# Another ring of score buffers, another order of batch 0, and another ending in a gather and scatter kernel

## The chip, the cores and the metric

The kernel runs on one core of one Trainium2 chip. The metric is device microseconds of one execution. The kernel before takes 828.68 us as the median of 3 runs (828.26 to 828.69). Times inside the execution are counted from the start of the profiled span. VectorE (DVE), ScalarE (ACT), GpSimd (POOL), TensorE (PE) and SyncE (SP) have instruction queues of their own; transfers between memory and the core's buffers are moved by 16 DMA engines, which serve SP's queue and GpSimd's queue.

## The reference

There are B = 8 batches. `scores` has 8 x 2048 x 2048 float32 numbers (134 MB), `values` and the output have 8 x 2048 rows of 2560 float32 numbers (10,240 bytes a row).

```python
best_j = np.argmax(scores, axis=2)
gathered = values[b_idx, best_j, :].copy()
out = np.zeros_like(values)
np.add.at(out, (b_idx, best_j, slice(None)), gathered)
```

So output row j of batch b is `values[b, j]` times the number of score rows of that batch whose maximum stands in column j. A row that is chosen once is a plain copy of its values row, one that is never chosen is zeros, and one that is chosen twice or more is the values row times its count. With the inputs of this case, batch 0 has 748 rows of the first kind, 761 of the second and 539 of the third, and the other batches differ from these by a few per cent.

## The kernel before

**Scores to counts** (`count_steps`, L166). A row tile is 128 score rows, one per partition, so a batch has NT = 16 row tiles and the kernel 128 of them; in this text they are numbered 0 to 127. SP loads two row tiles at a time (R = 2, 2 MB, 16,384 bytes per partition; L181), the very first load alone in two halves. VectorE finds the maximum of each row (L188) and its column (L189). After every four row tiles it makes one-hot matrices of the columns (L194 to L202), and TensorE adds them up into the batch's counts (L207).

**Where the scores lie.** NB = 7 buffers of two row tiles each are a rotating pool (`spool`). At the start three more stand in `vbig`, the area of six rows per partition that later stages gathered rows. For the first 20 loads (row tiles 0 to 39) buffers are taken in turn from all ten, so 20 row tiles can be there at once; afterwards 14 can. A load waits until VectorE has finished the tiles that its buffer held.

**Counts to output rows** (`value_steps`, L272). After a batch's counts are there, VectorE makes three kinds of index list, and GpSimd issues indirect transfers with them, 128 list entries a piece; an entry out of bounds moves no row.

- Single rows: 16 copies from DRAM to DRAM (`copy_once`, L285, issued at L33), one for each 128 rows, with an index out of bounds where the row isn't a single one. They need only the counts (L275 to L282).
- Zero rows: `zeros` (L369) writes a row of zeros to up to 7 x 128 listed rows (12 lists in the last batch). The lists come from a ranking (L294 to L355) in which TensorE has two short parts.
- Rows chosen more than once: `gathers` (L359) fetches up to 5 x 128 values rows into slots of `vbig` (L150), ScalarE multiplies each by its count (L363), and a scatter writes them (L155). There are six slots, so a gather waits for the scatter that used its slot.

VectorE, TensorE, ScalarE and SP run in the order in which the program is written (`manual_schedule`, L395). `count_steps` and `value_steps` are generators: at each `yield` of the first, after one row tile, the main loop (L397 to L406) lets the second, of the batch before, go on to its own next `yield`. For batches 0 and 1 the main loop takes four steps of `value_steps` at once (L404), so that all lists are made before the next batch's first row tile. For batch 0 GpSimd's order is 6 copies, then 7 zero lists with 7 copies between them, then 5 gathers with the last 3 copies between them, then 5 scatters; the gathers need the three `vbig` buffers back from the score tiles, and ten `yield`s (L380) put them behind row tiles in program order. For later batches 6 (batch 1) or 4 copies go first.

**The end.** Copies, zero lists and the last six scatters are marked `free_running` (L141): the framework doesn't follow them, and each adds 16 to a semaphore `landed`. At the end GpSimd waits until all have landed and resets its DMA state (L454 to L456). A branch before it (L421) handles inputs whose lists overflow and isn't taken here.

Of the kernel before, what the change touches and what calls it, by code (L numbers as in the profile page):

```python
# [8 lines left out]
FP32 = mybir.dt.float32  # L9
# [5 lines left out]
P = 128  # L15
# [21 lines left out]
def kernel(  # L37
# [6 lines left out]
    nc = tc.nc  # L44
    B, S, S2 = scores.shape
    _, _, H = values.shape
    assert S == S2
    NT = S // P
    BIG = float(1 << 24)
    R = 2  # L50
    G = 4
    NV = 6
    NX = NV * H // (R * S)
    NB = 7
    NM = NT // 2
    NE = 16
    LE = P // NE
    ZCAP, MCAP = 7, 5
# [6 lines left out]
    last_row = nc.gpsimd.to_reg(B * S - 1)  # L65

    consts = ctx.enter_context(tc.tile_pool(name="consts", bufs=1))
    spool = ctx.enter_context(tc.tile_pool(name="spool", bufs=NB))
    small = ctx.enter_context(tc.tile_pool(name="small", bufs=3))
    fin = ctx.enter_context(tc.tile_pool(name="fin", bufs=2))  # L70
    ohp = ctx.enter_context(tc.tile_pool(name="ohp", bufs=1))
# [44 lines left out]
    zero1 = consts.tile([P, 1], FP32)  # L116
# [2 lines left out]
    zrow = ctx.enter_context(nc.sbuf_tensor([P, H], FP32))  # L119
    nc.scalar.copy(zrow[:], zero1[:].to_broadcast([P, H]))  # L120

    vbig = ctx.enter_context(nc.sbuf_tensor([P, NV * H], FP32))
    nc.scalar.copy(vbig[:, NX * R * S:NV * H], zero1[:].to_broadcast([P, NV * H - NX * R * S]))

    ones_i = ctx.enter_context(nc.sbuf_tensor([P, B * NT], INT32))
    zero_i = ctx.enter_context(nc.sbuf_tensor([P, B * NT], INT32))
# [11 lines left out]
    landed = tc.alloc_semaphore("landed")  # L138
    n_free = [0]
# [14 lines left out]
    def scatter(v, idx, note=writes_out):  # L154
        note(nc.gpsimd.indirect_dma_start(  # L155
            out=out_flat[:, :], out_offset=bass.IndirectOffsetOnAxis(ap=idx, axis=0),
            in_=v, in_offset=None, bounds_check=B * S - 1, oob_is_err=False))

    vslot = [0]

    def stage():
        v = vbig[:, vslot[0] * H:(vslot[0] + 1) * H]
        vslot[0] = (vslot[0] + 1) % NV
        return v

    def count_steps(b, cnt_ps):  # L166

        am = None
        for u in range(NT // R):
            x = b * NT // R + u  # L170
            if x < 2 * (NX + NB) and x % (NX + NB) < NX:
                x %= NX + NB
                s_tile = vbig[:, x * R * S:(x + 1) * R * S]
            else:
                s_tile = spool.tile([P, R * S], FP32, name="s_tile")[:]
            rows_in = scores[b, u * R * P:(u + 1) * R * P, :].rearrange("(p r) s -> p (r s)", r=R)

            parts = R if b == u == 0 else 1
            for r in range(parts):
                part = slice(r * R * S // parts, (r + 1) * R * S // parts)  # L180
                nc.sync.dma_start(out=s_tile[:, part], in_=rows_in[:, part])  # L181
            if u * R % G == 0:
                am = small.tile([P, G, 8], U32, name="am")
            for r in range(R):
                g = (u * R + r) % G
                rows = s_tile[:, r * S:(r + 1) * S]
                mx = small.tile([P, 8], FP32)
                nc.vector.max(out=mx[:], in_=rows)  # L188
                nc.vector.max_index(out=am[:, g, :], in_max=mx[:], in_values=rows)  # L189
                if g < G - 1:  # L190
                    yield
            if (u + 1) * R % G == 0:
                lo = small.tile([P, G], U32)
                nc.vector.tensor_single_scalar(out=lo[:], in_=am[:, :, 0], scalar=P - 1, op=ALU.bitwise_and)  # L194
                hi = small.tile([P, G], U32)
                nc.vector.tensor_single_scalar(out=hi[:], in_=am[:, :, 0], scalar=7, op=ALU.logical_shift_right)  # L196
                oh_lo = small.tile([P, G, P], BF16)
                nc.vector.tensor_tensor(  # L198
                    out=oh_lo[:], in0=lo[:].unsqueeze(2).to_broadcast([P, G, P]),
                    in1=lane_f[:].unsqueeze(1).to_broadcast([P, G, P]), op=ALU.is_equal)  # L200
                oh_hi = small.tile([P, G, NT], BF16)
                nc.vector.tensor_tensor(  # L202
                    out=oh_hi[:], in0=hi[:].unsqueeze(2).to_broadcast([P, G, NT]),
                    in1=lane_f[:, 0:NT].unsqueeze(1).to_broadcast([P, G, NT]), op=ALU.is_equal)
                for g in range(G):
                    t = (u + 1) * R - G + g
                    nc.tensor.matmul(out=cnt_ps[:], lhsT=oh_lo[:, g, :], rhs=oh_hi[:, g, :],  # L207
                                     start=(t == 0), stop=(t == NT - 1))
                yield

    def level_engines(rank):

# [59 lines left out]
    def value_steps(b, cnt_ps):  # L272
# [14 lines left out]
                nc, out_flat[:, :], values[b, t * P:(t + 1) * P, :], one_i[:, t:t + 1], last_row))  # L287


        first = 6 if b < 2 else 4  # L290
        for t in range(first):
            copy_once(t)

# [22 lines left out]
        if b == B - 1:  # L316
# [9 lines left out]
            out=oh[:], in0=lo[:].unsqueeze(2).to_broadcast([P, NT, P]),  # L326
# [4 lines left out]
            out=ez[:], in0=hi[:, 0, :].unsqueeze(2).to_broadcast([P, NT, NT]),  # L331
# [3 lines left out]
            out=em[:], in0=hi[:, 1, :].unsqueeze(2).to_broadcast([P, NT, NM]),  # L335
# [6 lines left out]
        for t in range(NT):  # L342
            nc.tensor.matmul(out=l_ps[:], lhsT=oh[:, t, :], rhs=put[:, t, :], start=(t == 0), stop=(t == NT - 1))  # L343
        yield
        yield

        mi = many_i[:, b * NM:(b + 1) * NM]
        mc = many_c[:, b * NM:(b + 1) * NM]
# [8 lines left out]
        staged = []  # L357

        def gathers():  # L359
            for k in range(MCAP):  # L360
                v = stage()
                gather(v, mi[:, k:k + 1])
                nc.scalar.activation(out=v, in_=v, func=mybir.ActivationFunctionType.Copy, bias=0.0,  # L363
                                     scale=mc[:, k:k + 1])
                staged.append(v)
                if rest:
                    copy_once(rest.pop(0))

        def zeros(columns):  # L369
            for k in columns:  # L370
                scatter(zrow[:], zi[:, k:k + 1], free_running)
                if rest:
                    copy_once(rest.pop(0))
# [3 lines left out]
        if b == 0:  # L377
            zeros(range(nz))

            for _ in range(10):  # L380
                yield
            gathers()
        else:
            gathers()
            zeros(range(ZHEAD))
        for k in range(MCAP):

            scatter(staged[k], mi[:, k:k + 1], writes_out if b * MCAP + k < B * MCAP - NV else free_running)
        if b > 0:
            zeros(range(ZHEAD, nz))  # L390
        assert not rest
# [3 lines left out]
    with tc.manual_schedule(engines={ET.PE, ET.DVE, ET.Activation, ET.SP}):  # L395
        pending = iter(())
        for b in range(B):  # L397
            cnt_ps = psum_c.tile([P, NT], FP32)
            for _ in count_steps(b, cnt_ps):
                next(pending, None)  # L400
            for _ in pending:
                pass
            pending = value_steps(b, cnt_ps)
            if b < 2:  # L404
                for _ in range(4):
                    next(pending)  # L406
        for _ in pending:
            pass
        full = fin.tile([1, 2], FP32)
        nc.vector.tensor_reduce(out=full[:, 0:1], in_=tots[0:1, 0, 0:B - 1], op=ALU.max, axis=mybir.AxisListType.X)  # L410
        nc.vector.tensor_reduce(out=full[:, 1:2], in_=tots[0:1, 1, :], op=ALU.max, axis=mybir.AxisListType.X)
        over = fin.tile([1, 3], FP32)
        nc.vector.tensor_single_scalar(out=over[:, 0:1], in_=full[:, 0:1], scalar=float(ZCAP * P), op=ALU.is_gt)
        nc.vector.tensor_single_scalar(out=over[:, 1:2], in_=full[:, 1:2], scalar=float(MCAP * P), op=ALU.is_gt)
        nc.vector.tensor_single_scalar(out=over[:, 2:3], in_=most[0:1, :], scalar=float(ZLAST * LE), op=ALU.is_gt)
        over_i = fin.tile([1, 1], INT32)
        nc.vector.tensor_reduce(out=over_i[:], in_=over[:], op=ALU.max, axis=mybir.AxisListType.X)
# [3 lines left out]
    with tc.If(more > 0):  # L421

        n_spilt = 0
        last = nc.gpsimd.wait_ge(landed, 16 * n_free[0])
# [17 lines left out]
        for b in range(B):  # L442
            for k in range(MCAP, NM):
# [3 lines left out]
                with tc.issue_after(last.ins):  # L447
                    scaled = nc.gpsimd.tensor_scalar(
                        out=zrow[:], in0=zrow[:], scalar1=many_c[:, i:i + 1], scalar2=None, op0=ALU.mult)
# [1 line left out]
                with tc.issue_after(scaled.ins):  # L451
                    scatter(zrow[:], many_i[:, i:i + 1], one_by_one)

    last = nc.gpsimd.wait_ge(landed, 16 * n_free[0])  # L454
    with tc.issue_after(last.ins):
        nc.gpsimd.dma_reset()  # L456


# [28 lines left out]
```

## Time and profile before

| | |
|---|---|
| profiled execution | 828.68 us, of which the span is 826.9 us |
| DMA engines | 347.04 MB moved, mean 420 GB/s; busy in all 40 slices |
| GpSimd's DMA queue | 38,736 packets, 212.67 MB, 62.0% of the engines' span |
| SP's DMA queue | 9,360 packets, 134.22 MB, 38.2% |
| VectorE | busy 679.3 us (82%), in one piece until 695 us |
| GpSimd | busy 274.1 us (33%) |
| ScalarE, TensorE | 12%, 2% |
| TensorE's granted clock | 1.00 |

The table's shares are averages over the span. The page also has a strip of 40 slices of about 20.7 us each, with the busy tenths of each engine and the GB/s that the DMA engines moved. A "wait" row names who waited, for whom, the sum, how often and the longest. A "windows" row gives, for one stretch of the span, the busy time of each engine, the granted clock, the busy share of the DMA engines and their GB/s; a share may come out a little over 1, as packets overlap.

### The profile page before, as it was taken

The page shows a single profiled execution, that of the slowest core. Times are in us where ns is not written, and L with a number is a line of the kernel's source. Part 1 is how long each engine was busy: PE and PEld are TensorE (multiplying, and loading weights), DVE is VectorE, ACT ScalarE, POOL GpSimd, SP SyncE. Part 2 cuts the span into 40 slices and gives each one's busy share as a digit, 9 for nine tenths or more (in the row PEclk, how much of TensorE's full clock was granted, in tenths as well). Part 3 has the DMA queues.
Part 4 walks back from the last instruction along what each step waited for, and adds up shares of the span by engine and source line. Part 5 has one row for each costly group of instructions (what it writes and reads, how often), then busy time and mean ns, then how long its engine had stood idle before and what let it go on. Part 6 is the DMA issues. An engine that isn't in the chain of part 4 may idle for free.

```text
span 826.9 us, 2079 instructions
## 1 busy us (share of the span) xinstructions
PE 14.7 (2%) x273; PEld 14.2 (2%) x273; DVE 679.3 (82%) x794; ACT 103.0 (12%) x43; POOL 274.1 (33%) x277
## 2 busy tenths in 40 slices
PE   0000000000000000000000000000000000000000
PEld 0000000000000000000000000000000000000000
DVE  7999999999999999999999999999999996000000
ACT  3000000501210001220002300002200220230230
POOL 0000643157021160052330151511425356346442
DMA  9999999999999999999999999999999999999997
GB/s 380 430 426 430 372 423 422 425 411 422 423 425 428 428 427 430 425 427 427 429 424 426 426 430 430 422 429 426 427 426 423 424 427 422 425 424 424 422 427 295
DMA packets 48112, 347.04 MB, mean 420 GB/s; under 512 B 19014, under 2 KB 19014, under 8 KB 19014
## 3 DMA queue, kind: packets, MB, share of 16 engines
q0 software_dynamic: 38736, 212.67, 62.0%
q1 hardware_dynamic: 9360, 134.22, 38.2%
q14 instruction: 14, 0.11, 0.0%
q8 instruction: 2, 0.03, 0.0%
HBM read 354.42 MB, written 300.15 MB: 792 GB/s over the span
## 4 chain that ended last, share of the span: by engine, by line
DVE 43%; DMA 18%; issue 17%; POOL 11%; another core or an unknown queue 8%; PE 0%; POOLq 0%
DVE am L189 19%; DVE mx L188 18%; DMA vbig<-in_values_dram,many_i 14%; POOL out_dram L33 6%; DMA out_dram<-vbig,many_i 4%; POOL out_dram L155 4%; POOL vbig L150 2%; DVE oh_lo L198 1%; DVE oh L325 1%; DMA vbig<-in_scores_dram 1%; DVE lo L194 0%; DVE oh_hi L202 0%; PE l_ps L343 0%; DVE put L340 0%
## 5 line engine op out<-in xcount | busy, mean ns | idle before, releaser
L189 DVE FIND_INDEX8 am<-mx,s_tile 128x8 uint32<-128x2048 f32 x116 | 265.0, 2285 | 0.0
L188 DVE MAX8 mx<-s_tile 128x8 f32<-128x2048 f32 x116 | 264.3, 2278 | 0.0
L363 ACT ACTIVATE vbig<-vbig,many_c 128x2560 f32<-128x2560 f32 x40 | 96.8, 2426 | 692.7 <-DMA vbig<-in_values_dram,many_i 658.5
L33 POOL DMA_INDIRECT out_dram<-in_values_dram,ones_i x128 | 132.3, 1033 | 152.3 <-DVE m L296 114.3
L155 POOL DMA_INDIRECT out_dram<-vbig,many_i x40 | 39.3, 983 | 239.1 <-ACT vbig L363 236.3
L150 POOL DMA_INDIRECT vbig<-in_values_dram,many_i x40 | 41.9, 1048 | 126.8 <-DMA out_dram<-vbig,many_i 79.2
L155 POOL DMA_INDIRECT out_dram<-zrow,zero_i x61 | 59.5, 976 | 18.8 <-issue 18.8
L188 DVE MAX8 mx<-vbig 128x8 f32<-128x2048 f32 x12 | 27.3, 2279 | 4.8 <-DMA vbig<-in_scores_dram 4.8
L189 DVE FIND_INDEX8 am<-mx,vbig 128x8 uint32<-128x2048 f32 x12 | 27.4, 2284 | 0.0
L198 DVE TENSOR_TENSOR oh_lo<-lo,lane_f 128x512 bf16<-128x512 uint32 x32 | 22.3, 696 | 0.4
L325 DVE TENSOR_TENSOR oh<-lo,fill_f 128x2048 f16<-128x2048 uint32 x8 | 18.3, 2292 | 0.3
L207 PE MATMUL cnt_ps<-oh_hi,oh_lo 128*128 128x16 bf16 x128 | 8.2, 174 | 579.0 <-DVE oh_hi L202 529.4
L207 PEld LDWEIGHTS <-oh_lo 128*128 128x128 bf16 x128 | 8.4, 105 | 578.8 <-DVE oh_lo L198 577.8
L189 DVE MATCH_VALUE_LOAD am<-mx,s_tile 128x8 f32 x116 | 10.7, 92 | 4.0
L202 DVE TENSOR_TENSOR oh_hi<-hi,lane_f 128x64 bf16<-128x64 uint32 x32 | 7.0, 217 | 0.0
L194 DVE TENSOR_SCALAR lo<-am 128x4 uint32<-128x4 uint32 x32 | 5.8, 181 | 1.1
L343 PE MATMUL l_ps<-put,oh 128*128 128x32 f16 x128 | 4.7, 188 | 68.8 <-DVE put L340 68.8
L343 PEld LDWEIGHTS <-oh 128*128 128x128 f16 x128 | 4.7, 104 | 69.9 <-DVE oh L325 59.6
L196 DVE TENSOR_SCALAR hi<-am 128x4 uint32<-128x4 uint32 x32 | 5.4, 170 | 0.0
L351 DVE TENSOR_SCALAR e<-l_ps 128x32 f32<-128x32 f32 x8 | 1.5, 187 | 3.1 <-PE l_ps L343 3.1
L330 DVE TENSOR_TENSOR ez<-hi,lane_f 128x256 f16<-128x256 uint32 x8 | 3.3, 418 | 0.0
L340 DVE TENSOR_TENSOR put<-ez,row_f 128x256 f16<-128x256 f16 x8 | 3.3, 417 | 0.0
(91 smaller groups left out, 61.3 us busy)
## 6 DMA issues: line engine op xcount, KB each, us to landing
s_tile<-in_scores_dram SPq DMA_DIRECT2D x58, 2048.0 KB, 12.0
vbig<-in_scores_dram SPq DMA_DIRECT2D x5, 2048.0 KB, 37.3
vbig<-in_scores_dram SPq DMA_DIRECT2D x2, 1024.0 KB
out_dram<-in_values_dram,ones_i POOLq DMA_INDIRECT x128
out_dram<-zrow,zero_i POOLq DMA_INDIRECT x61
vbig<-in_values_dram,many_i POOLq DMA_INDIRECT x40, 33.0
out_dram<-vbig,many_i POOLq DMA_INDIRECT x40, 59.1
```

Of the source, the lines that this page charges most:

```text
L33: return eng.add_instruction(ins)
L150: note(nc.gpsimd.indirect_dma_start(out=v, out_offset=None, in_=values_flat[:, :], in_offset=bass.IndirectOffsetOnAxis(ap=idx, axis=0), bo ...
L155: note(nc.gpsimd.indirect_dma_start(out=out_flat[:, :], out_offset=bass.IndirectOffsetOnAxis(ap=idx, axis=0), in_=v, in_offset=None, bound ...
L188: nc.vector.max(out=mx[:], in_=rows)
L189: nc.vector.max_index(out=am[:, g, :], in_max=mx[:], in_values=rows)
L194: nc.vector.tensor_single_scalar(out=lo[:], in_=am[:, :, 0], scalar=P - 1, op=ALU.bitwise_and)
L198: nc.vector.tensor_tensor(out=oh_lo[:], in0=lo[:].unsqueeze(2).to_broadcast([P, G, P]), in1=lane_f[:].unsqueeze(1).to_broadcast([P, G, P]) ...
L202: nc.vector.tensor_tensor(out=oh_hi[:], in0=hi[:].unsqueeze(2).to_broadcast([P, G, NT]), in1=lane_f[:, 0:NT].unsqueeze(1).to_broadcast([P, ...
L207: nc.tensor.matmul(out=cnt_ps[:], lhsT=oh_lo[:, g, :], rhs=oh_hi[:, g, :], start=(t == 0), stop=(t == NT - 1))
L325: nc.vector.tensor_tensor(out=oh[:], in0=lo[:].unsqueeze(2).to_broadcast([P, NT, P]), in1=fill_f[:].unsqueeze(1).to_broadcast([P, NT, P]), ...
L343: nc.tensor.matmul(out=l_ps[:], lhsT=oh[:, t, :], rhs=put[:, t, :], start=(t == 0), stop=(t == NT - 1))
L363: nc.scalar.activation(out=v, in_=v, func=mybir.ActivationFunctionType.Copy, bias=0.0, scale=mc[:, k:k + 1])
```

## The change

One area `room` takes the place of `vbig` and the pool. It holds 21 row tiles at first (7 of them in the staging part) and 14 from row tile 42 on. `place` gives the position of a row tile, and a table `loads` says where a load begins and how many row tiles (1, 2, 3 or 4) it brings: 1 for row tiles 0, 1 and 36 to 41, 2 for tiles 2 and 3, and up to 4 elsewhere, as far as the places are adjacent and the batch isn't over. There are 43 loads instead of 65.

For batch 0, all 16 copies go before the zero lists. Its lists are made one step per row tile of batch 1 instead of all at once; the gathers stand behind row tile 27 (`tiles[0] < turn + NX`). Batch 1 keeps its four steps at once.

All scatters are followed by the framework again, and the wait on `landed` with the reset at the end is replaced by a drain of GpSimd.

```diff
-    R = 2
+    R = 4
-    NX = NV * H // (R * S)
-    NB = 7
+    NX = NV * H // S
+    NB = 14
...
-    spool = ctx.enter_context(tc.tile_pool(name="spool", bufs=NB))
...
-    vbig = ctx.enter_context(nc.sbuf_tensor([P, NV * H], FP32))
-    nc.scalar.copy(vbig[:, NX * R * S:NV * H], zero1[:].to_broadcast([P, NV * H - NX * R * S]))
+    room = ctx.enter_context(nc.sbuf_tensor([P, NV * H + NB * S], FP32))
+    nc.scalar.copy(room[:, 0:NV * H - NX * S], zero1[:].to_broadcast([P, NV * H - NX * S]))
+    turn = NX + NB
+
+    def place(x):
+
+        return NV * H + (x % turn - NX if x < 2 * turn else (x - 2 * turn) % NB) * S
+
+    loads, x = {}, 0
+    while x < B * NT:
+        n = 1
+        most_n = 1 if x < 2 or 2 * turn - 6 <= x < 2 * turn else 2 if x < 4 else R
+        while n < most_n and (x + n) % NT and place(x + n) == place(x) + n * S:
+            n += 1
+        loads[x] = n
+        x += n
...
+        for t in range(NT):
+            x = b * NT + t
+            if x in loads:
+                n = loads[x]
+                nc.sync.dma_start(out=room[:, place(x):place(x) + n * S],
+                                  in_=scores[b, t * P:(t + n) * P, :].rearrange("(p r) s -> p (r s)", r=n))
...
+            rows = room[:, place(x):place(x) + S]
...
-        first = 6 if b < 2 else 4
+        first = (NT, 6, 4)[min(b, 2)]
...
         yield
-        yield
+        if b > 0:
+            yield
...
-            for _ in range(10):
+            while tiles[0] < turn + NX:
                 yield
             gathers()
...
-            scatter(staged[k], mi[:, k:k + 1], writes_out if b * MCAP + k < B * MCAP - NV else free_running)
+            scatter(staged[k], mi[:, k:k + 1])
...
-            if b < 2:
-                for _ in range(4):
-                    next(pending)
+            for _ in range((1, 4, 0)[min(b, 2)]):
+                next(pending)
...
-    last = nc.gpsimd.wait_ge(landed, 16 * n_free[0])
-    with tc.issue_after(last.ins):
-        nc.gpsimd.dma_reset()
+    nc.gpsimd.drain()
```

More of the change, by code (lines that the diff above doesn't have):

```diff
@@ L159 @@
     vslot = [0]
+    tiles = [0]
     def stage():
-        v = vbig[:, vslot[0] * H:(vslot[0] + 1) * H]
+        v = room[:, vslot[0] * H:(vslot[0] + 1) * H]
         vslot[0] = (vslot[0] + 1) % NV
@@ L168, in count_steps @@
         am = None
[L169 to L182, printed above, removed]
-                am = small.tile([P, G, 8], U32, name="am")
[L184 to L190, printed above, removed]
-                    yield
-            if (u + 1) * R % G == 0:
+        for t in range(NT):
[4 more added lines that the diff above has]
+                                  in_=scores[b, t * P:(t + n) * P, :].rearrange("(p r) s -> p (r s)", r=n))
+            g = t % G
+            if g == 0:
+                am = small.tile([P, G, 8], U32, name="am")
+            rows = room[:, place(x):place(x) + S]
+            mx = small.tile([P, 8], FP32)
+            nc.vector.max(out=mx[:], in_=rows)
+            nc.vector.max_index(out=am[:, g, :], in_max=mx[:], in_values=rows)
+            if g == G - 1:
                 lo = small.tile([P, G], U32)
@@ L204, in count_steps @@
                     in1=lane_f[:, 0:NT].unsqueeze(1).to_broadcast([P, G, NT]), op=ALU.is_equal)
[L205 to L209, printed above, removed]
+                for k in range(G):
+                    nc.tensor.matmul(out=cnt_ps[:], lhsT=oh_lo[:, k, :], rhs=oh_hi[:, k, :],
+                                     start=(t == G - 1 and k == 0), stop=(t == NT - 1 and k == G - 1))
+            tiles[0] = x + 1
+            yield
     def level_engines(rank):
@@ L344, in value_steps @@
         yield
-        yield
+        if b > 0:
+            yield
         mi = many_i[:, b * NM:(b + 1) * NM]
```

## The prediction

> **What bounds the kernel now.** I read the page's strip first. VectorE works until slice 34 and then stops, while the DMA engines are busy in every slice and move 422 to 430 GB/s in nearly all: the kernel ends when the last bytes have moved, and VectorE, 130 us early, isn't the bound.
>
> ```profile
> DVE  7999999999999999999999999999999996000000
> DMA  9999999999999999999999999999999999999997
> GB/s 380 430 426 430 372 423 422 425 411 422 423 425 428 428 427 430 425 427 427 429 424 426 426 430 430 422 429 426 427 426 423 424 427 422 425 424 424 422 427 295
> ...
> q0 software_dynamic: 38736, 212.67, 62.0%
> q1 hardware_dynamic: 9360, 134.22, 38.2%
> ```
>
> The change moves the same bytes. It can only alter what a byte costs, and the stretches in which some DMA engine has nothing to move. Those show as slices under 422: the start, the fifth (372), the ninth (411) and the last (295). Windows cut around them (last column GB/s, the one before it the DMA share):
>
> ```profile
> 12.00:80.00 68.00, 0.76 (x12) 0.79 (x12) 67.45 (x56) 0.00 (x0) 0.00 (x0) 1.00 1.01 429
> 86.00:106.00 20.00, 0.78 (x18) 0.69 (x17) 18.59 (x31) 0.00 (x0) 15.71 (x15) 1.00 0.97 367
> 106.00:171.00 65.00, 0.77 (x12) 0.79 (x12) 64.38 (x56) 12.14 (x5) 18.83 (x19) 1.00 1.01 424
> 171.00:180.00 9.00, 1.06 (x22) 0.98 (x22) 7.26 (x31) 0.00 (x0) 6.24 (x5) 1.00 0.99 417
> 180.00:190.00 10.00, 0.00 (x0) 0.00 (x0) 9.93 (x7) 0.00 (x0) 7.56 (x9) 1.00 1.01 386
> 815.00:826.90 11.90, 0.00 (x0) 0.00 (x0) 0.00 (x0) 0.00 (x0) 0.00 (x0) 1.00 0.52 201
> ```
>
> Against 427, the first dip costs (427-367) x 20/427 = 2.8 us, and 171 to 190 costs 0.2 + 1.0 = 1.2 us. Both follow a batch end at which VectorE makes lists for some 8 us and frees no score buffer, so loads run out, while GpSimd issues copies at one per 1.28 us; a copy of batch 0 carries 748/16 = 47 rows = 0.48 MB, hence at most 376 GB/s. The last window is the tail: 11.9 x 201/427 = 5.6 us of full work, so the average engine ends at 820.6 and the last bytes move by 825. The engine that has waited most sets the end, 4 us behind the average.
>
> GpSimd's waits and the timeline around batch 0 give the dates:
>
> ```profile
> 86.03 1.11 POOL L33 DMA_INDIRECT out_dram<-in_values_dram,ones_i  x1 [84.29 <-DVE m L296]
> ...
> 122.14 1.04 POOL L150 DMA_INDIRECT vbig<-in_values_dram,many_i  x1 [8.74 <-DVE am L189]
> ...
> 142.18 1.00 POOL L150 DMA_INDIRECT vbig<-in_values_dram,many_i  x1 [4.12 <-DVE am L189]
> ...
> 165.42 0.97 POOL L155 DMA_INDIRECT out_dram<-vbig,many_i  x1 [2.42 <-ACT vbig L363]
> 172.54 0.98 POOL L33 DMA_INDIRECT out_dram<-in_values_dram,ones_i  x1 [6.16 <-DVE m L296]
> ```
>
> Between 165.4 and 172.5 GpSimd has nothing left of batch 0 to issue. What fills the DMA engines there in the kernel before are score loads: by the trace SP issues two row tiles at 150.57 (tile 27 done), two at 160.83 (tile 29) and two at 170.01 (tile 31).
>
> **The change, term by term.** The profiled execution took 828.68 us, which is also the median, so the sum starts there (span 826.9 + 1.8 around it).
>
> *1. The average engine, up to 190 us.* A row tile is 1.049 MB, 2.44 us at 429 GB/s. Tile 0 is there at 5.9 us (the first maximum starts at 5.88), so at 86.0 some 33.8 tiles have landed in either kernel. In the new ring row tile 42 comes back to the pool part, and its load of four waits for tile 31, done at 170.0 as now: VectorE's work isn't changed, only its list work moves behind tile 16. So until then the loads have 42 - 33.8 = 8.2 tiles = 8.6 MB, and GpSimd has batch 0: 748 + 761 + 2 x 539 = 2587 rows = 26.5 MB. Together 35.1 MB may move from 86 to 171. The kernel before moved 20 x 0.367 + 65 x 0.424 = 34.9 MB in that time, the engines could do 85 x 0.427 = 36.3. So the new kernel fills the first dip (16 copies, 7 zero lists and single-tile loads queue up without a pause, and lists made between tiles 16 and 18 are ready at about 103, before the last copy is issued at 86 + 16 x 1.28 = 106.5), and pays with a new hole before 171 of up to 1.2 MB or 2.8 us: a gain of only 0.2 MB, 0.5 us. From 171 to 190 four row tiles (9.8 us) lie beside batch 1's copies, and the 1.2 us of that dip is gained. Sum -1.7 us.
>
> *2. The engine that sets the end.* The copies of batch 0 aren't even: the program books copies by partition groups of eight (L104 to L109), and counted so from the inputs the 748 rows split into 35 to 60 per engine, mean 46.75. The poorest is 11.75 rows short, x 0.385 us a row (10,240 bytes at 427/16 GB/s) = 4.5 us. In the new hole nothing is left for it, whereas in the kernel before four row tiles (9.8 us) reach it between 150 and 171. Its extra loss is 0 if the old dips already hit it as hard, 4.5 if not at all. I take 3.0: those loads lie where it runs dry, while the old dips cost the average engine 4.0. Later batches have their own poor engines, and the program evens out only the totals, at the very end.
>
> *3. The chain of batch 0's rows.* Three more copies (3 x 1.13 us) lie before the gathers, and the gathers need row tiles of 2048, not pairs: the third to fifth wait for tiles 24, 25 and 26 (136.8, 141.4, 146.0) instead of 23, 24 and 25. Each scatter then waits for landing and for ScalarE's 2.43 us, behind the last engine to land. That leaves part of a scatter (1.3 MB, 3.1 us) to be moved after 171 in place of before: 0 to 3.1 us, I take 0.7, as the fourth and fifth scatter are now issued only at 162 and 165 and GpSimd ends no later.
>
> *4. Four-tile loads later.* A load is issued when four tiles are free, not two, so at any time up to two tiles (4.9 us) less has been asked for. It costs only where GpSimd's queue also runs low: before batch 2's lists, where GpSimd waits 23.8 us for counts and 16.2 us more for lists ("POOL vbig L150 <- DVE many_c L355: 16.2, 1, 16.2"). Now the engines keep 428 GB/s there. Bounds 0 and 4.9; I take 0.9, near the row without a dip. VectorE itself has ten tiles (46 us) ahead at each issue, against 12.0 us median landing of 2 MB loads, and 130 us of slack.
>
> *5. Packets.* The queue table gives two equations: 0.382 x 826.9 x 16 us for 134.22 MB in 9,360 packets, 0.620 x 826.9 x 16 us for 212.67 MB in 38,736. They solve to 0.0371 ns a byte and 8.2 ns a packet. 65 loads are 65 x 128 row packets and 65 x 16 small ones (= 9,360); 43 loads drop 22 x 144 = 3,168: 1.6 us per engine. But packets overlap (share 1.01), so the gain is 0 to 1.6; I take 0.8.
>
> *6. The end.* The wait and reset end with a DRAIN of 299 ns at 825.7 and a plain one of 53 ns at 826.0. The new drain depends on no transfer, and the built program has it at the head of GpSimd's queue; what ends the kernel is the framework's own drain. Without the reset 0.3 us go, but that plain drain now meets untidied transfers: at most the 2.2 us from last packet to span end again. -0.3 to +2; I take 0.
>
> Sum: -1.7 + 3.0 + 0.7 + 0.9 - 0.8 + 0 = +2.1, 830.8 us.
>
> **Where a rule bears on it.** Loads land in a median of 12.0 us, gathers in 33.0, both on engines that are full at 427 GB/s. The Trainium skill ("DMA: Bandwidth & Descriptors", Queues, rings and completion order) says that a DMA engine takes turns between queues packet by packet; the 16,384-byte packets would then have 62% beside GpSimd's 10,240 bytes, and packets of 32,768 bytes 76%. That speaks against the change, as gathers land later; by it term 3 would rise from 0.7 towards 3.1. [...]
>
> **The rivals.** (a) *It cancels.* If the old dips hit the poor engines as hard as the new hole (term 2 at 0 to 1.5), the sum is -0.9 to +0.6: 827.8 to 829.3. Speaking for it: the share of 0.97 in the old dip is an average too. (b) *Faster*: the hole before 171 doesn't open or is even, and the dips are gained whole: -4.0 - 0.8 = 823.9, or with term 1 alone -1.7 - 1.6 - 0.3 = 825.1. It decides if 148 to 171 stays above about 415 GB/s. Against it stands the ledger, where 1.2 MB are missing. (c) *The end no longer waits* for the untracked transfers: after the last scatter (issued 796.8) stand 8 zero lists and 3 copies, so the program would be over when GpSimd has issued them (811.8) plus 1.2 us, 813 instead of 826.9: 815 us. Against it: a framework's drain still stands behind them. (d) *VectorE becomes the bound* through late loads: only past 130 us of lost time; no chance.
>
> **How the numbers follow.** A measurement of this kernel tells about 0.2% (1.7 us) from no change. Forecast case, slower by over that, 830.4 to about 834: 0.43. (a) with small sums on both sides of it: 0.33. (b) 0.20. (c) 0.04, counted as faster. The low end takes (b)'s middle, 825.0; the high end is the sum with term 2 at 4.5 and term 4 at 2: 828.68 - 1.7 + 4.5 + 0.7 + 2 - 0.8 = 833.4, and 834 with a little of term 6. The forecast case's own range is 830.4 to 834.
>
> **What would show it.** Right: 86 to 106 near 420 GB/s; a hole at 148 to 171, about 395 to 410 over that stretch; SP's load of 42 to 45 at 170.0; 171 to 190 full; SP's queue with about 6,190 packets; last bytes some 2 us later, at nearly the same average end. Wrong: no hole (the ledger misses work), a second dip at 270 to 290 of more than 2 us (term 4), or an end before GpSimd's last transfers have landed.

## The result, and the profile after

| | before | after |
|---|---|---|
| time, median | 828.47 us (827.90 to 828.69) | 832.15 us (831.55 to 832.53) |
| profiled execution | 828.68 us, span 826.9 | 832.21 us, span 830.4 |

The changed kernel is slower: ratio 1.0045, 95% interval 1.0027 to 1.0062, that is 3.7 us (2.2 to 5.1). The forecast was slower by 2.1 us. The side is right, but the profile shows that the time was lost at another place than where the forecast put it.

The page of the changed kernel, strip and queues:

```profile
DVE  7999999999999999999999999999999994000000
DMA  9999999999999999999999999999999999999995
GB/s 380 448 431 425 405 411 423 410 396 412 429 427 428 413 431 434 433 417 426 425 429 431 429 430 423 419 434 424 429 427 419 424 427 421 425 426 424 424 426 222
...
q0 software_dynamic: 38736, 212.67, 61.7%
q1 hardware_dynamic: 6192, 134.22, 37.8%
```

The fifth slice has risen from 372 to 405, so the first dip is partly filled; the ninth has fallen from 411 to 396. SP's queue has 6,192 packets, as forecast. The last slice has fallen from 295 to 222, and this is the first sign: the slices are 20.8 us long, the same bytes are moved, and the tail has grown.

Windows of the changed kernel, the last two columns being the DMA share and GB/s:

```profile
86.00:106.00 20.00, 0.78 (x18) 0.68 (x17) 19.62 (x30) 0.00 (x0) 15.82 (x14) 1.00 1.00 404
106.00:148.00 42.00, 0.51 (x8) 0.53 (x8) 41.62 (x35) 0.00 (x0) 13.75 (x14) 1.00 1.02 420
148.00:171.00 23.00, 0.51 (x8) 0.53 (x8) 22.31 (x29) 12.03 (x5) 4.88 (x5) 1.00 0.96 392
171.00:180.00 9.00, 0.80 (x18) 0.71 (x18) 7.76 (x24) 0.00 (x0) 7.41 (x6) 1.00 1.01 433
180.00:190.00 10.00, 0.00 (x0) 0.00 (x0) 9.90 (x9) 0.00 (x0) 7.56 (x9) 1.00 0.98 376
270.00:290.00 20.00, 0.84 (x20) 0.84 (x20) 19.76 (x26) 0.00 (x0) 5.81 (x6) 1.00 1.01 414
```

Two of the same stretches in the kernel before:

```profile
148.00:171.00 23.00, 0.25 (x4) 0.26 (x4) 22.73 (x23) 9.71 (x4) 3.90 (x4) 1.00 1.01 425
270.00:290.00 20.00, 0.84 (x20) 0.84 (x20) 19.79 (x24) 0.00 (x0) 4.37 (x5) 1.00 1.02 427
```

In all six, the kernel before moved 367, 424, 425, 417, 386 and 427 GB/s. Priced at 427 as in the prediction: 86 to 106 gains (404-367) x 20/427 = 1.7 us, 106 to 148 loses 0.4, 148 to 171 loses (425-392) x 23/427 = 1.8, 171 to 190 gains 0.1, and 270 to 290 loses 0.6. That is a net loss of 1.0 us. The average engine nevertheless ends no later (below), so something outside these windows makes up for it: from 12 to 80, where only loads run, the rate rose from 429 to 432 GB/s, worth 0.5 us, which fits fewer packets but isn't shown to come from them. None of this is where 3.7 us went.

The 3.7 us lie behind the last byte. The windows of the end, first of the kernel before, then of the changed one:

```profile
815.00:820.00 5.00, 0.00 (x0) 0.00 (x0) 0.00 (x0) 0.00 (x0) 0.00 (x0) 1.00 0.91 367
820.00:825.00 5.00, 0.00 (x0) 0.00 (x0) 0.00 (x0) 0.00 (x0) 0.00 (x0) 1.00 0.33 111
825.00:831.00 6.00, 0.00 (x0) 0.00 (x0) 0.00 (x0) 0.00 (x0) 0.00 (x0) 1.00 0.00 0
```

```profile
815.00:820.00 5.00, 0.00 (x0) 0.00 (x0) 0.00 (x0) 0.00 (x0) 0.00 (x0) 1.00 0.89 353
820.00:825.00 5.00, 0.00 (x0) 0.00 (x0) 0.00 (x0) 0.00 (x0) 0.00 (x0) 1.00 0.32 111
825.00:831.00 6.00, 0.00 (x0) 0.00 (x0) 0.00 (x0) 0.00 (x0) 0.00 (x0) 1.00 0.00 0
```

Both kernels have moved their last byte before 825 (the last packet is recorded at 824.7 and 824.5 us). The average engine ends at 815 + 5 x (367+111)/427 = 820.6 before and 815 + 5 x (353+111)/427 = 820.4 after. But the span ends at 826.9 before and at 830.4 after. What stands between is in the rows of GpSimd's closing instructions (durations as shortest/median/longest in ns, then the first and last start in us). Before, the reset's drain (L456) and the framework's drains (L482):

```profile
L456 POOLq DRAIN  x1: 299/299/299, 825.7 to 825.7; - x1
```

```profile
L482 POOLq DRAIN  x3: 40/53/94, 826.0 to 826.6; - x3
```

After, the drain that the change wrote (L459) and the framework's drains (L485):

```profile
L459 POOLq DRAIN  x1: 909/909/909, 0.9 to 0.9; - x1
```

```profile
L485 POOLq DRAIN  x3: 40/113/21970, 807.6 to 830.1; - x3
```

The drain in the source ran at 0.9 us, ahead of all of GpSimd's transfers, and has nothing to do with the end. The framework's own drain is recorded from 807.6 us, while GpSimd still carries out its last issues, and takes 21.97 us, to 829.6. The last transfer's increments are recorded at 825.7 in both kernels. So the drain holds the end for another 3.9 us after everything has landed; the wait and the reset before took 0.3 us there.

### The profile page after: what moved, and what is told of

Read it like the earlier page. It is cut to its first block, busy times and chain, and to the rows that moved or that the text cites. A ratio compares the mean times of both kernels' runs of the same rounds, so it can differ in the third digit from the quotient of the medians.

```text
span 830.4 us, 2035 instructions
## 1 busy us (share of the span) xinstructions
PE 14.7 (2%) x273; PEld 14.1 (2%) x273; DVE 679.0 (82%) x794; ACT 101.3 (12%) x43; POOL 275.7 (33%) x277
## 3 DMA queue, kind: packets, MB, share of 16 engines
q1 hardware_dynamic: 6192, 134.22, 37.8%
## 4 chain that ended last, share of the span: by engine, by line
DVE 71%; DMA 13%; issue 8%; POOL 6%; another core or an unknown queue 1%; POOLq 0%; PE 0%; DVEq 0%
DVE am L197 32%; DVE mx L196 30%; DMA room<-in_values_dram,many_i 8%; DMA out_dram<-room,many_i 4%; POOL out_dram L33 3%; DVE oh_lo L204 2%; POOL out_dram L170 2%; DVE oh L331 2%; POOL room L165 1%; DVE lo L200 1%; DMA room<-in_scores_dram 1%; DVE oh_hi L208 0%; DVE hi L202 0%; DVE put L346 0%
## 5 line engine op out<-in xcount | busy, mean ns | idle before, releaser
L196 DVE MAX8 mx<-room 128x8 f32<-128x2048 f32 x128 | 291.6, 2278 | 4.6 <-DMA room<-in_scores_dram 4.6
L197 DVE FIND_INDEX8 am<-mx,room 128x8 uint32<-128x2048 f32 x128 | 292.5, 2285 | 0.0
L370 ACT ACTIVATE room<-room,many_c 128x2560 f32<-128x2560 f32 x40 | 96.8, 2427 | 693.2 <-DMA room<-in_values_dram,many_i 693.1
L170 POOL DMA_INDIRECT out_dram<-room,many_i x40 | 40.7, 1019 | 238.6 <-ACT room L370 235.8
L165 POOL DMA_INDIRECT room<-in_values_dram,many_i x40 | 42.1, 1053 | 120.5 <-DMA out_dram<-room,many_i 71.9
L197 DVE MATCH_VALUE_LOAD am<-mx,room 128x8 f32 x128 | 11.8, 92 | 4.3
L321 DVE TENSOR_SCALAR rank<-base,off_ps 128x16 f32<-128x16 f32 x16 | 3.0, 241 | 0.0
L344 DVE TENSOR_TENSOR put<-em,row_f 128x128 f16<-128x128 f16 x8 | 2.3, 292 | 0.3
## 6 DMA issues: line engine op xcount, KB each, us to landing
room<-in_values_dram,many_i POOLq DMA_INDIRECT x40, 32.9
```

What stands on the lines that cost most here:

```text
L165: note(nc.gpsimd.indirect_dma_start(out=v, out_offset=None, in_=values_flat[:, :], in_offset=bass.IndirectOffsetOnAxis(ap=idx, axis=0), bo ...
L170: note(nc.gpsimd.indirect_dma_start(out=out_flat[:, :], out_offset=bass.IndirectOffsetOnAxis(ap=idx, axis=0), in_=v, in_offset=None, bound ...
```

## The experiments

Theory 1 after this reading: the ending costs the whole 3.5 us, and the ring and batch 0's order cancel. Theory 2 is the prediction's: the poorest engine and the later loads cost 2 to 3 us. The second group asks what the drain does, the third where the gain of ring and order went. All times in one group of runs stand beside the kernel before on the same chip.

**The ending alone, from both sides.** The changed kernel with the old ending:

```diff
-            scatter(staged[k], mi[:, k:k + 1])
+            scatter(staged[k], mi[:, k:k + 1], writes_out if b * MCAP + k < B * MCAP - NV else free_running)
...
-    nc.gpsimd.drain()
+    last = nc.gpsimd.wait_ge(landed, 16 * n_free[0])
+    with tc.issue_after(last.ins):
+        nc.gpsimd.dma_reset()
```

> The changed kernel with the old ending (last six scatters not followed, wait for the count of landed transfers, reset). Theory 1, the ending is the whole loss: in the profiles the last packet moves at 824.7 us before and 824.5 after, but the span ends 2.2 us behind it before and 5.9 us behind it after, because the framework's drain of GpSimd met transfers that were still out. Then this kernel ends 2.2 us behind its last packet and takes 828.3 to 828.6, the same as the kernel before. Theory 2, the prediction's: the poorest engine and the later loads cost 2 to 3 us; then the last packet is late, and this kernel takes 830.5 to 832.

And the kernel before with the new ending, the same lines the other way round:

> The kernel before with the new ending alone (all scatters followed, a drain in place of the wait and the reset). Theory 1: last packet at 824.7 as before, the framework's drain ends some 4 us behind the last landing, 828.5 + 3.5 = 832.0. Theory 2: the ending is worth 0 within 0.5 us: 828.2 to 829.0.

Measured beside 828.32 us for the kernel before: the changed kernel with the old ending 828.59 (ratio 1.0003, 0.9994 to 1.0012), the kernel before with the new ending 831.82 (1.0041, 1.0028 to 1.0055). The ending is worth 832.15 - 828.59 = 3.6 us on one side (3.4 if each is first compared with the kernel before of its own group) and 831.82 - 828.32 = 3.5 on the other. In the second, the long drain is there with nothing else changed:

```profile
L480 POOLq DRAIN  x3: 40/113/20668, 808.4 to 829.6; - x3
```

Theory 1 holds, theory 2 falls.

**Is it the missing wait, or the missing reset?** The wait put back, without the reset:

```diff
-    nc.gpsimd.drain()
+    nc.gpsimd.wait_ge(landed, 16 * n_free[0])
```

(with the last six scatters `free_running`, as above).

> The changed kernel, with the wait for the landed transfers put back, but no reset. Rivals on what costs 3.5 us at the end. 1a: the framework's drain is slow because transfers are still out when it is issued; with the wait in front of it nothing is out, it takes 0.1 us, and the kernel takes 828.3 to 828.8. 1b: the drain has to tidy up behind every transfer, whether landed or not, unless the reset has thrown that away; then it starts at 825.7, ends 3.5 to 4 us later, and the kernel takes 832 as without the wait.

Measured: 835.72 us (1.0085, 1.0071 to 1.0099), slower still by 3.6 us than the changed kernel. The drain now starts when nothing is out, and it isn't short:

```profile
L485 POOLq DRAIN  x3: 40/108/7675, 825.9 to 834.1; - x3
```

So it isn't a wait for transfers under way. The drain has some 7.7 us of work behind landed transfers, and it is the reset that makes it needless. 1b is right about what costs, but said 832: with the wait in front, none of that work can lie beside the last transfers, which would explain why the wait alone is worse than the bare drain (this reason is argued, see the last section).

**The written drain.** Only the last line of the change removed:

```diff
-    nc.gpsimd.drain()
```

> The changed kernel without its last line, the drain that the change wrote. By the profile that drain ran at 0.9 us, at the head of GpSimd's queue, for 0.9 us, and the framework's own drain stands at the end in either case. Theory 1: nothing changes, 831.8 to 832.5. Rival: the drain that was written is the one that is slow, or the two together are; then 828.3 to 828.8.

Measured: 832.02 us beside 828.25 (1.0055, 1.0033 to 1.0076), as with the line. It does nothing for the time.

**What the drain's length goes with.** The wait without the reset, and the copies of seven batches left out:

```diff
         def copy_once(t):
+            if b < 7:
+                return
```

> The changed kernel with the wait for landed transfers but no reset, and with the 112 copies of batches 0 to 6 left out, so that GpSimd issues 157 indirect transfers and not 269; those rows are not written. Its time says nothing; the length of the framework's drain does. With 269 transfers landed it took 7.68 us. If it tidies up after every transfer since the start, it takes 7.68 x 157 / 269 = 4.5 us. If its length is fixed, by the queues or their rings, it stays at 7.7 us. If only the transfers of the last stretch count, it also stays near 7.7, as batch 7 and all zero lists, gathers and scatters are the same.

```profile
L487 POOLq DRAIN  x3: 40/108/4817, 769.5 to 774.8; - x3
```

4.82 us behind 157 transfers, where 7.68 us stood behind 269: it grows with the transfers since the start, at 30.7 and 28.5 ns each. (A transfer has 144 packets in both runs, so that transfers and packets can't be told apart.) To tell "since the start" from "not tidied yet", the kernel with the wait and no reset got one more drain halfway:

```diff
         assert not rest
+        if b == 3:
+            with tc.issue_after(newest[0].ins):
+                nc.gpsimd.drain()
```

(`newest[0]` is the last transfer marked `free_running`).

> The changed kernel with the wait for landed transfers and no reset, and one more drain of GpSimd halfway, issued behind batch 3's last transfer. By the two drains measured so far (7.68 us behind 269 transfers, 4.82 us behind 157) a drain costs 25.5 ns for each transfer since the start, and 0.8 us. If the cost is for transfers not tidied yet, the midway drain takes over 132 of them, and the last one, behind the other 137, takes 0.8 + 137 x 0.0255 = 4.3 us. If every drain goes through all transfers since the start, the last one still takes 7.7 us. If the midway drain also waits until its transfers have landed, it stands in GpSimd's queue for some 30 us, and the stretch from about 440 to 480 us is short of transfers.

The midway drain (L403) and the framework's (L491):

```profile
L403 POOLq DRAIN  x1: 67772/67772/67772, 472.5 to 472.5; - x1
```

```profile
L491 POOLq DRAIN  x3: 46/108/3904, 850.3 to 854.8; - x3
```

The last drain takes 3.90 us behind 137 transfers (28.5 ns each; 4.3 was expected): the midway one has taken over the rest. It also waits for its transfers: it is recorded for 67.8 us, from 472.5 to 540.3, instead of the 30 expected, and the engines move nothing from 538 until GpSimd has issued again at 541.0. GpSimd still issues until 478.2 under the drain's record, so it stands for 62.9 us. Toward the end of that time the engines run dry:

```profile
520.00:540.00 20.00, 0.84 (x20) 0.84 (x20) 19.65 (x31) 0.00 (x0) 0.00 (x0) 1.00 0.59 241
```

where the same kernel without it moves 418 GB/s. The span grew from 834.4 to 855.1 us (one execution with the midway drain). So here a drain in the middle is no way to spread the cost.

**Ring and order, each alone.** All of the following have the old ending. The ring with batch 0's old order:

```diff
-        first = (NT, 6, 4)[min(b, 2)]
+        first = 6 if b < 2 else 4
...
-        if b > 0:
-            yield
+        yield
...
-            for _ in range((1, 4, 0)[min(b, 2)]):
+            for _ in range((4, 4, 0)[min(b, 2)]):
```

> The changed kernel with the old ending, 6 copies first in batch 0 and its lists made at once before row tile 16, as in the kernel before; the gathers stay behind row tile 27, as the 21-tile ring needs it. So the ring, the grain and the gathers' place are new, the order of copies and lists is old. (The run e6 had the gathers two row tiles earlier, where they wrote over row tiles 26 and 27 before these had been read: its counts are others and its time isn't used.) If the new order closes the dip at 86 to 106 by itself, this kernel has about 370 to 390 GB/s there and takes 829 to 830; if the single loads of 36 to 41 close it, the stretch stays near 404 and the kernel takes 828.3 to 828.9, as with the new order.

A first attempt at this kernel, e6, also had the ten `yield`s of the kernel before in place of the condition on row tile 27:

> The changed kernel with the old ending and batch 0 in its old order (6 copies first, lists made at once before row tile 16, gathers ten row tiles later), so only the ring and its loads are new. Reference: 828.59 with the new order. If the new order has closed the dip at 86 to 106 (367 to 404 GB/s, 1.7 us) and the hole at 148 to 171 (1.9 us) is the grain's, this kernel has both: 829.5 to 830.5. If the hole is the price of the new order, which has given GpSimd's work away earlier, this kernel has the old dip and no hole, and takes the same, 828.2 to 828.9.

It took 854.24 us, but its gathers wrote over row tiles 26 and 27 before these were read (VectorE waits 25.1 us for a product of ScalarE's that lies where it reads scores), so that its lists are others, and the time says nothing on the question.

And the kernel before with the new order alone:

```diff
-        first = 6 if b < 2 else 4
+        first = (NT, 6, 4)[min(b, 2)]
...
-        yield
+        if b > 0:
+            yield
...
-            for _ in range(10):
+            for _ in range(8):
                 yield
...
-            if b < 2:
-                for _ in range(4):
-                    next(pending)
+            for _ in range((1, 4, 0)[min(b, 2)]):
+                next(pending)
```

> The kernel before with the new order of batch 0 alone (16 copies first, lists one step per row tile, gathers behind row tile 25 as before), old buffers, loads of two and old ending. By the prediction's ledger, here the score loads up to 171 us are not short (46 - 33.8 = 12.2 row tiles = 12.8 MB, and 26.5 MB of batch 0, where the engines could move 36.3 MB), so that no hole opens at 148 to 171 (420 GB/s or more), and 86 to 106 gains what earlier loads of 36 and 37 bring, some 10 to 30 GB/s = 0.5 to 1.4 us: 826.9 to 827.8. If the order is what opens the hole, that gain is lost again at 148 to 171: 828 to 829.

Measured beside 828.58 us: the ring alone 829.93 (1.0016, 1.0007 to 1.0025), the order alone 829.31 (1.0008, 0.9999 to 1.0017). Together they were 828.59 beside 828.32. Windows of the ring alone, of the order alone, and of both (the first experiment):

```profile
86.00:106.00 20.00, 0.78 (x18) 0.69 (x17) 18.63 (x29) 0.00 (x0) 15.73 (x15) 1.00 0.99 388
106.00:148.00 42.00, 0.52 (x8) 0.53 (x8) 41.62 (x36) 0.09 (x1) 13.62 (x14) 1.00 1.02 424
148.00:171.00 23.00, 0.43 (x8) 0.52 (x8) 22.52 (x21) 11.94 (x5) 5.27 (x5) 1.00 0.97 396
171.00:190.00 19.00, 0.87 (x21) 0.71 (x18) 17.45 (x36) 0.00 (x0) 14.15 (x13) 1.00 0.95 386
```

```profile
86.00:106.00 20.00, 0.78 (x18) 0.69 (x17) 19.61 (x33) 0.00 (x0) 15.96 (x14) 1.00 0.94 356
106.00:148.00 42.00, 0.50 (x8) 0.52 (x8) 41.62 (x35) 0.72 (x1) 13.83 (x15) 1.00 1.01 416
148.00:171.00 23.00, 0.51 (x8) 0.52 (x8) 22.32 (x25) 11.31 (x5) 5.16 (x5) 1.00 1.01 425
171.00:190.00 19.00, 0.80 (x18) 0.71 (x18) 17.65 (x33) 0.00 (x0) 14.60 (x14) 1.00 1.02 410
```

```profile
86.00:106.00 20.00, 0.78 (x18) 0.69 (x17) 19.64 (x30) 0.00 (x0) 15.75 (x14) 1.00 1.00 404
106.00:148.00 42.00, 0.51 (x8) 0.53 (x8) 41.62 (x35) 0.00 (x0) 13.72 (x14) 1.00 1.01 419
148.00:171.00 23.00, 0.51 (x8) 0.52 (x8) 22.31 (x29) 12.03 (x5) 4.87 (x5) 1.00 0.96 393
171.00:190.00 19.00, 0.81 (x18) 0.72 (x18) 17.60 (x31) 0.00 (x0) 15.00 (x14) 1.00 1.00 407
```

These are one profile each. The hole at 148 to 171 comes with the ring (396 and 393) and not with the order (425), which is where the ledger of row tiles puts it. The dip at 86 to 106 needs both: the ring alone lifts it from 367 to 388, the order alone lowers it to 356, together they make 404. Summed against 427 over these windows and 270 to 290 (427, 412, 426 and 414 GB/s for before, ring, order and both), the losses are 4.4, 6.3, 5.3 and 5.2 us. With 0.8 us taken off for fewer packets wherever the ring is (the prediction's estimate, not a measurement), that makes +1.1, +0.9 and 0.0 against before; the medians were +1.35, +0.73 and +0.27. So the windows give the size and order of the medians. They don't carry each execution: the three profiled ones stand at +1.3, +2.0 and -0.7 against the profile of before, so that about 1 us of the order's loss, and a gain of 0.7 us with both, lie elsewhere. And with an interval from 0.9999, the order's cost isn't clear of none. My expectation of 829 to 830 for the ring fits, with its reason half right: the ring, with its single loads, does close a part of the dip. For the order, 826.9 to 827.8 fails, and so does the rival of 828 to 829: there was no hole, but the dip was deeper.

**The grain.** Row tiles 42 to 45 loaded one by one, and then all loads at most two row tiles:

```diff
-        most_n = 1 if x < 2 or 2 * turn - 6 <= x < 2 * turn else 2 if x < 4 else R
+        most_n = 1 if x < 2 or 2 * turn - 6 <= x < 2 * turn + 4 else 2 if x < 4 else R
```

> The changed kernel with the old ending, and row tiles 42 to 45 loaded one by one instead of in one load of four. In the changed kernel 148 to 171 us moved 392 GB/s instead of 425, worth 1.9 us, because that load waits for row tile 31 (168.5). If the grain of that load alone makes the hole, the four loads go out at about 154, 159, 163.6 and 168.5, the stretch is back at 415 or more, and the kernel gains 1 to 1.8 us on the same kernel with the load of four: 826.7 to 827.5. If the hole only moves behind 171, or the engine that ends last is another, it gains nothing: 828.3 to 828.6.

```diff
-    R = 4
+    R = 2
```

> The changed kernel with the old ending and loads of at most two row tiles (R = 2), so the ring, the single loads of 36 to 41 and the order of batch 0 stay and only the grain of four goes. Terms 4 and 5 of the prediction set a cost of 0.9 us for late loads of four against a gain of 0.8 us for fewer packets. Reference: the same kernel with loads of four took 828.59. If the dip at 270 to 290 (414 GB/s in place of 427, 0.6 us) and part of the hole at 148 to 171 come from the grain, they close and the kernel gains up to 1.5 us less 0.8 for packets: 827.4 to 828.6. If the packets outweigh, 829 to 829.5.

Measured: single loads 828.51 us beside 828.32 (1.0000, 0.9991 to 1.0009), pairs 828.66 beside 828.25 (1.0004, 0.9995 to 1.0013). Neither moves the time. With pairs, 270 to 290 is back:

```profile
270.00:290.00 20.00, 0.84 (x20) 0.84 (x20) 19.76 (x26) 0.00 (x0) 6.04 (x6) 1.00 1.02 427
```

and 12 to 80, where only loads run, falls from 432 to 428 GB/s: the dip of 0.6 us is the price of the grain, and the faster loads there (68 x 4/428 = 0.6 us) make up for it. With single loads the first goes out at 154.84 instead of 168.50, and yet the hole stays:

```profile
148.00:171.00 23.00, 0.51 (x8) 0.52 (x8) 22.32 (x28) 12.14 (x5) 4.87 (x5) 1.00 0.98 386
```

The share is higher (0.98) with fewer bytes: the loads' packets of 8,192 bytes took 357 ns there on average, in place of 315 at 106 to 148. More work on offer didn't fill the hole, and why its packets took longer isn't settled. So a lack of loads, the ledger's reason for the hole, isn't shown to be its cause.

No variant beats both kernels by more than the measurement can tell. The changed kernel with the old ending can't be told from the kernel before and is 3.6 us ahead of the changed one.

## Why the prediction was right, and where it was wrong

It forecast slower, and the time lies in its range, for the wrong reason. Terms 1 to 5 were to bring +2.1 us and brought +0.3 (-0.5 to +1.0); term 6 was taken at 0 and brought +3.5. That the total fits is luck: a cost of 3.0 us that never came (term 2) stood in for one of 3.5 that wasn't counted (term 6).

1. *The average engine, -1.7.* The ledger held in sum: by the windows 20 x 0.404 + 42 x 0.420 + 23 x 0.392 = 34.7 MB moved from 86 to 171, under its limit of 35.1, though single loads, which put up to three more row tiles in reach, left the hole at 386 GB/s. But the step "the new kernel fills the first dip" was too large (404, not 420), and the hole's 392 was just under "395 to 410". That "the 1.2 us of that dip is gained" from 171 to 190 failed: the load of four is nearly through by 181 (its last packet ends at 183.3), the next one goes out at 187.4, and the copies all but alone bring 376 GB/s there, which is the figure the prediction itself had worked out for copies. By the windows the term came out at +0.4.
2. *The engine that sets the end, +3.0.* This failed. The last packet stands 4.1 us behind the average end before (824.7 and 820.6) and 4.1 after (824.5 and 820.4): the term is 0. Its lower bound, "0 if the old dips already hit it as hard", was the right value. The sign that the prediction named for it, "last bytes some 2 us later", didn't come: they came 0.2 us earlier. Which engine ends last wasn't measured.
3. *The chain of batch 0's rows, +0.7.* The fourth and fifth scatter went out at 162.33 and 164.65 (before: 162.04 and 165.42), and the load of 42 to 45 at 168.54 (170.0 was forecast). The term's cost can't be told apart from the hole's. That gathers land later is half true: over all of them the median is 32.9 us, against 33.0 before, but batch 0's first gather, issued at 121.30, let ScalarE start at 150.53, 29.2 us later, and before it was 20.9 (122.14 to 143.04). With the order alone it was 26.2 (121.04 to 147.28), so most of this comes with the order. The prediction weighed the Trainium skill here ("DMA: Bandwidth & Descriptors", Queues, rings and completion order: an engine takes turns between queues, packet by packet), by which it expected larger load packets to make gathers land later. No run here shows that: the loads moved beside this gather were single row tiles, with packets of 8,192 bytes in place of 16,384. Besides, a packet of that page is a group of typically 9 to 17 descriptors, and the prediction's shares of 62% and 76% put one row's packet of the profile in its place; no run shows how the two are related.
4. *Four-tile loads later, +0.9.* Right in place and near in size: 0.6 us at 270 to 290, and gone with pairs.
5. *Packets, -0.8.* Consistent: pairs bring back the dip's 0.6 us and gain nothing.
6. *The end, 0 (-0.3 to +2).* This is the step that failed most: the bound of the framework's drain. It saw that the framework's drain would meet untidied transfers, and bounded that by "the 2.2 us from last packet to span end". That row says nothing of it: in the kernel before, the reset had thrown the work away, and the drain's 53 ns are the price of having nothing to do. The honest bound from the trace of before would have been open upwards. Measured: 3.5 us.

Of the rivals, (a), that it cancels, is what the ring and the order did; (b) falls with 392 GB/s, under its 415; (c), an end that no longer waits, is the opposite of what happened, since the framework's drain waits and works; (d) never came near: VectorE stops 130 us before the end.

## What to carry to other kernels

A duration in the old profile prices an operation only in the state that the old kernel put it in: a 53 ns drain behind a reset says nothing of the same drain without the reset, and an instruction at the end of the source may be issued at the start. When a kernel ends on its last bytes, look at the stretch between the last packet and the end of the span first; it can be read off the windows, and here it held the whole result. Two changes can be worse apart than together: here the ring alone was 1.35 us slower and the order alone 0.73 (not clear of none), both 0.27, and only both filled the first dip to 404 GB/s. So test them apart and together before keeping either.

## What the runs showed of the hardware that was not expected

GpSimd's drain at the end has work for every indirect transfer that it has issued and that no drain or reset has dealt with: 7.68 us behind 269, 4.82 behind 157, 3.90 behind 137, some 28 to 31 ns each, with all of them landed. A reset behind a wait takes its place in 0.30 us. Without the wait, the drain stands in the queue while the last transfers move, and only 3.9 us of it are left behind the last landing, so the bare drain (832.15 us) beats a wait without a reset (835.72). It may work on the early transfers in the meantime, which would explain this. The midway drain fits that: with 132 transfers ahead of it, 3.8 us at 28.5 ns each, it ended only some 2 us after the last packet (538.2 to 540.3). But no run shows it directly. In mid-kernel a drain also waits for what GpSimd has in flight: its record lasts 67.8 us, from 472.5 us on, and the engines have stopped moving bytes when it ends.
